# Row sums of squares for an RMS norm: from a transposed copy with adds and matmuls to the tokens' own layout with an accumulating activation

## The chip, the cores and the metric

The kernel runs on one core of one Trainium2 chip. The metric is the device time of one execution in microseconds (us); the figure for a version is the median of several runs. The engines are named as the profile names them: PE is TensorE (PEld its weight loads), DVE is VectorE, ACT is ScalarE, POOL is GpSimd, and SP is the engine whose queue issues most of the DMAs. Each engine, and the SP queue too, takes its instructions in the order in which the program lists them.

## The reference

One layer of a backbone over 2048 latent tokens and 256 context tokens, each a row of 1024 fp32 numbers. What matters here is its first step, cut from the reference:

```python
def _rmsnorm(x, g):
    xf = x.astype(jnp.float32)
    xf = xf * lax.rsqrt(jnp.mean(xf * xf, axis=-1, keepdims=True) + EPS)
    return (xf * g.astype(jnp.float32)).astype(x.dtype)
...
        mod = jax.nn.silu(c) @ w_ada[i] + b_ada[i]
        mod_c = jax.nn.silu(c_ctx) @ w_ada[i] + b_ada[i]
...
        h_lat = _rmsnorm(x, norm_g[i]) * (1.0 + scale) + shift
        h_ctx = _rmsnorm(ctx, norm_g[i]) * (1.0 + scale_c) + shift_c
...
    na_q, na_k, na_v, na_g, r_q, r_k, r_v, r_g = _split_proj(h_lat @ w_in)
```

So each token needs the sum of the squares of its own 1024 numbers before its row of h can be formed, and h is what the big projection h @ w_in reads. Behind it come neighbourhood attention, retention, an output projection and a last norm; the change does not touch those.

## The kernel before

**Groups and blocks.** The tokens are handled in nine groups of 256: group i = 0 to 7 is latent tokens, group 8 the context. A block is what the projection takes as one operand: blocks 0 to 3 are two groups each (block 2 is groups 4 and 5, block 3 is groups 6 and 7), block 4 is group 8. PE multiplies h in two parts: `hi`, a rounded copy (tiles `hhi`, and `chi` for the context), and `lo`, the rest (tiles `hlo`, `clo`). Both must be ready for a row block k of a block before PE can use it.

**What is done to a group.** Its data come transposed (features on partitions, tokens along the row) by `load_x`, two DMAs of 512 KB. Then, by the short names that the plan uses:

- `sq` squares: ACT squares both halves into two `st` tiles (L198); for one half POOL, for the other DVE adds the four feature blocks together (L200, L201), and DVE adds the two halves (L203).
- `cs` colsum: PE multiplies the result by a column of ones (L209), which sums over the partitions and leaves one sum for each token in PSUM.
- `rs` rstd and spread_copy: DVE scales the sum (L214), POOL takes the power -1/2 (L215), DVE copies it along a row (L220).
- `sp` spread: PE turns that into a row for every partition (L227, two matmuls of 128 for each group).
- `mu`: DVE multiplies the transposed data with it (L241). `ab`: DVE (L272) and ACT (L274) apply scale and shift. `hl`: ACT casts to `hi` (L279), POOL or DVE subtracts for `lo` (L283), and the raw data are queued to be stored to DRAM for a later pass (`spill_step`, L253). Groups 0 and 1 go through `p` (prep_first) instead, one feature block k at a time: cast on ACT (L262), scale and shift on DVE (L263), `lo` on DVE or POOL (L265).

**The order.** Nothing is reordered by a scheduler. PE works through five windows, one for each block (L363), a window having 32 steps of three matmuls of 512 columns. After step n (counted over all windows, so that window 1 begins with step 32, window 2 with 64, window 3 with 96) the program lists the actions whose entry in the table `PLAN` has this n: `(52, 'sq', 6)` puts the squares of group 6 behind step 52 on every engine that they use. The times at which an engine gets to them depend on what stands ahead of them in its own queue. The modulation matmuls over `w_ada` (`m`, L311, with `ar` and `af`) are in the same plan, for the first 16 steps. A finished unit of a window is cast by ACT (L383), its rest is taken by DVE (L384) and both go out by one DMA on SP (`kS`, L151). Of the `o` tiles for that there are two.

**Buffers and queues.** `st` tiles of 512 KB are four, taken in turn by weights, squares and the context data. The DMAs of SP are issued in program order, and each waits for the landing of the one eight places ahead of it in the queue.

Of the kernel before, what the change touches and what calls it, by code (L numbers as in the profile page):

```python
# [9 lines left out]
F32 = mybir.dt.float32  # L10
BF16 = mybir.dt.bfloat16
F32R = mybir.dt.float32r
AF = mybir.ActivationFunctionType
# [5 lines left out]
P = 128  # L19
# [39 lines left out]
]  # L59
SPL = [9, 0, 1, 0]  # L60
ALO = [0, 5, 9, 4]
# [21 lines left out]
def hybrid_kernel(ctx: ExitStack, tc: tile.TileContext, a: dict, out: bass.AP):  # L83
    nc = tc.nc
# [33 lines left out]
    def pool(st, name, bufs, **kw):  # L118
        return st.enter_context(tc.tile_pool(name=name, bufs=bufs, reuse_waits="tile", **kw))
# [9 lines left out]
    psm = pool(ctx, "psm", 2, space=PSUM)  # L129
    KH = KC // 2  # L130
    env = dict(pp=pool(psx, "pp", 6, space=PSUM), st=pool(sx, "st", 4, side="right"), queue=nc.sync)

    def ptile(p=None):
        return (p or env["pp"]).tile([P, 512], F32, name="mm")
# [23 lines left out]
    blk = [(hx.tile([P, KC, 512], F32R, name="hhi"), hx.tile([P, KC, 512], F32R, name="hlo"))] + [None] * 4  # L158
# [4 lines left out]
    xsq = [[xraw[4 + i][:, u * KH:(u + 1) * KH, :] for u in range(2)] for i in range(2)]  # L163
# [27 lines left out]

    sqs, rms, rbs, prs = {}, {}, {}, {}

    def squares(i):
        sqs[i] = []
        for u in range(2):
            sq = xsq[i][u] if i < 2 else env["st"].tile([P, KH, 256], F32, name="st")
            nc.scalar.activation(sq, raw[i][u], AF.Square)  # L198
            eng = (nc.gpsimd, nc.vector)[u]
            eng.tensor_tensor(sq[:, 0:2, :], sq[:, 0:2, :], sq[:, 2:4, :], ALU.add)  # L200
            eng.tensor_tensor(sq[:, 0, :], sq[:, 0, :], sq[:, 1, :], ALU.add)  # L201
            sqs[i].append(sq)
        nc.vector.tensor_tensor(sqs[i][0][:, 0, :], sqs[i][0][:, 0, :], sqs[i][1][:, 0, :], ALU.add)  # L203

    def colsum(*ii):
        pm = ptile(None if ii[0] < 4 else psm)
        for j, i in enumerate(ii):
            for t in range(2):
                nc.tensor.matmul(pm[:, 2 * j + t:2 * j + t + 1], sqs[i][0][:, 0, t * P:(t + 1) * P], one, start=True, stop=True)  # L209
            rms[i] = pm[:, 2 * j:2 * j + 2]  # L210

    def rstd(i):
        r = env["st"].tile([P, 2], F32, name="rs", bufs=4)
        nc.vector.tensor_scalar(r, rms[i], 1.0 / D, EPS, ALU.mult, ALU.add)  # L214
        nc.gpsimd.tensor_tensor(r, r, mhalf[:, 0:2], ALU.pow)  # L215
        rbs[i] = r

    def spread_copy(i):
        rbs[i, 1] = env["st"].tile([P, 2, P], F32, name="t0", bufs=2)
        nc.vector.tensor_copy(rbs[i, 1], rbs[i].unsqueeze(2).to_broadcast([P, 2, P]))  # L220

    def spread(*ii):
        pm = ptile()
        for j, i in enumerate(ii):
            prs[i] = pm[:, j * 256:(j + 1) * 256]
            for t in range(2):
                nc.tensor.matmul(prs[i][:, t * P:(t + 1) * P], rbs[i, 1][:, t, :], ident, start=True, stop=True)  # L227
# [10 lines left out]
    def spread_mul(i, uu=(0, 1)):  # L238
        for u in uu:
            x = raw[i][u]  # L240
            nc.vector.tensor_tensor(x, x, prs[i].unsqueeze(1).to_broadcast([P, KH, 256]), ALU.mult)  # L241
# [93 lines left out]
    def w_raw(c0):  # L335
        return st_halves(a["w_in"][c0 // WG])
# [14 lines left out]
    def w_split(rw, lo=3):  # L351
        w, parts = w_parts(rw, lo)
        for p in parts:
            p()
        return w
# [108 lines left out]
    lds = dict(a=ada_load, x=load_x, c=small, w=lambda g: wr.append(w_raw(512 + 256 * g)))  # L464
    for name, *args in LOADS:
        lds[name](*args)
    acts = dict(sq=squares, cs=lambda *i: colsum(*i), rs=lambda i: (rstd(i), spread_copy(i)), sp=lambda *i: spread(*i),
                mu=lambda i, u: spread_mul(i, (u,)), ab=prep_ab, hl=prep_hl, blk=alloc_blk, x=load_x, w=lambda: wr.append(w_raw(2560)),
                w2=lambda: load_w(), s=ada_split, m=ada_mm, ar=ada_row, af=ada_fin, p=prep_first,
                ws=lambda g: w01.append(w_split(wr[g], lo=WSL[g])))  # L470
# [16 lines left out]
    def load_w():  # L487
        if wseq:
            wcur.append(w_raw(wseq.pop(0)))
# [523 lines left out]
    def dims(t):  # L1013
        h, i, j = t // 16, t // 4 % 4, t % 4
        return h, i, j, KWIN[i][0], KWIN[i][1], CWIN[j][0], CWIN[j][1]
# [214 lines left out]
    for t in range(NT + 3):  # L1230
# [27 lines left out]
        h, i, j = dims(t)[:3]  # L1258
# [237 lines left out]
    q, r = divmod(48 - used, 7)  # L1496
# [127 lines left out]
```

## Time and profile before

| | us |
|---|---|
| median of three runs | 1363.7 |
| lowest and highest run | 1363.22, 1367.48 |
| the profiled execution | 1366.09 |
| its span, from the first to the last instruction | 1364.1 |

All times inside the profile count from the start of that span; 2.0 us of the profiled execution lie outside it, and it is 2.4 us above the median of the runs. In the lists of instructions a row gives start, length, engine, line, operation, out<-in, how many were merged, and in brackets the idle time of the engine just before it with what ended it. An engine name with q (SPq) means the issue of a DMA, not its transfer. PEclk is the share of the full TensorE clock that was granted.

### The profile page before, as it was taken

Reading aid. Unit: us, or ns where it says so; the run is one execution under the profiler, and the core shown is the slowest. Engines: PE = TensorE matmul, PEld = TensorE weight load, DVE = VectorE, ACT = ScalarE, POOL = GpSimd, SP = SyncE. Lnnn points to the kernel's source line nnn. Section 1 sums busy time; section 2 is a strip of 40 time slices with the busy share of each in tenths; the row PEclk is TensorE's granted clock in tenths of the full one; section 3 lists DMA queues with packets and bytes.
Section 4 is the critical chain, followed back from the end, with each engine's and each line's share of the span. In section 5 each row is a group of like instructions: output and inputs, shape, how many; then the busy total and the mean of one; then the engine's idle time right before and its main releaser. Section 6 shows DMA issues by size and latency. Waiting matters only on the chain.

```text
span 1364.1 us, 23087 instructions
## 1 busy us (share of the span) xinstructions
PE 1313.1 (96%) x8236; PEld 1148.9 (84%) x8236; DVE 827.9 (61%) x1442; ACT 606.5 (44%) x1259; POOL 583.8 (43%) x571
## 2 busy tenths in 40 slices
PE   6999999999999999999999999999999899999997
PEld 2477899887997788998999889889998789888886
DVE  5686356675766754377767777776644633445345
ACT  5354343243533344555655466556642234333332
POOL 5452102554034664355535465555422254544432
PEclk9999999999999999999999999999999999999999
DMA  9386788464867657967587778676538988455533
GB/s 364 132 277 232 260 296 222 165 208 151 326 179 228 217 197 230 273 198 194 157 225 208 210 202 245 171 215 188 140 110 277 267 264 286 159 170 170 162 121 128
DMA packets 197685, 287.25 MB, mean 211 GB/s; under 512 B 17345, under 2 KB 126017, under 8 KB 196290
## 3 DMA queue, kind: packets, MB, share of 16 engines
q1 hardware_dynamic: 165154, 228.35, 56.4%
q10 hardware_dynamic: 32416, 57.42, 11.7%
q8 instruction: 66, 1.08, 0.3%
q14 instruction: 49, 0.40, 0.1%
HBM read 194.48 MB, written 91.23 MB: 209 GB/s over the span
## 4 chain that ended last, share of the span: by engine, by line
PE 70%; DMA 9%; DVE 8%; ACT 4%; POOL 3%; issue 3%; SPq 2%; ACTq 0%; POOLq 0%; DVEq 0%
PE mm L374 17%; PE mm L671 13%; PE mm L1465 11%; PE mm L363 7%; PE sS L1025 4%; PE tr L1052 3%; PE po L1073 3%; PE mm L1188 2%; PE tr L1054 2%; PE po L1075 2%; DMA vB<-o 1%; PE mm L1377 1%; PE mm L1376 1%; PE mm L1375 1%; PE mm L311 1%
## 5 line engine op out<-in xcount | busy, mean ns | idle before, releaser
L374 PE MATMUL mm<-whi,hlo 128*128 128x256 f32 x832 | 228.5, 282 | 0.2 <-DMA hlo<-cS 0.2
L374 PE MATMUL mm<-whi,hhi 128*128 128x256 f32 x768 | 224.2, 292 | 0.0
L374 PE MATMUL mm<-wlo,hhi 128*128 128x256 f32 x768 | 216.9, 282 | 0.0
L1056 ACT CAST pt<-tr 128x640 fp32r<-128x640 f32 (+1 forms) x128 | 95.6, 747 | 160.9 <-PE tr L1054 158.4
L1062 DVE TENSOR_TENSOR pt<-tr,pt 128x640 fp32r<-128x640 f32 (+1 forms) x128 | 113.9, 890 | 78.5 <-ACT pt L1056 77.2
L374 PEld LDWEIGHTS mm<-whi,hlo 128*128 128x128 f32 x832 | 156.3, 190 | 0.6 <-DMA hlo<-cS 0.5
L1045 POOL TENSOR_SCALAR sp<-sp,stt 128x640 f32<-128x640 f32 (+2 forms) x128 | 103.2, 808 | 106.5 <-DVE stt L1044 74.5
L374 PEld LDWEIGHTS mm<-whi,hhi 128*128 128x128 f32 x768 | 146.2, 190 | 0.0
L374 PEld LDWEIGHTS mm<-wlo,hhi 128*128 128x128 f32 x768 | 145.9, 190 | 0.1
L1034 DVE CUSTOM_DVE_ANT_0 sp<-sS,nb 128x640 f32<-128x640 f32 (+2 forms) x128 | 105.6, 825 | 33.6 <-PE sS L1025 27.2
L1039 ACT ACTIVATE sp<-sp,stt 128x640 f32<-128x640 f32 (+2 forms) x128 | 107.4, 839 | 19.9 <-DVE stt L1034 18.7
L625 POOL TENSOR_TENSOR whi<-st,whi 128x512 fp32r<-128x512 f32 x48 | 63.9, 1353 | 107.3 <-ACT whi L624 107.3
L363 PE MATMUL mm<-hhi,whi 128*128 128x512 f32 x256 | 107.8, 421 | 0.0
L363 PE MATMUL mm<-hlo,whi 128*128 128x512 f32 x256 | 101.6, 397 | 6.0 <-DVE hlo L265 2.1
L1025 PE MATMUL sS<-k,q 128*128 128x256 f32 (+3 forms) x512 | 99.0, 315 | 5.3 <-DVE stt L1034 5.0
L363 PE MATMUL mm<-hhi,wlo 128*128 128x512 f32 x256 | 101.9, 398 | 0.3 <-DVE wlo L347 0.3
L671 PE MATMUL mm<-hhi,whi 128*128 128x512 f32 x336 | 98.4, 395 | 3.7 <-POOL whi L625 3.2
L1474 DVE TENSOR_TENSOR xt<-mm,xt 128x512 f32<-128x512 f32 x64 | 43.8, 686 | 87.4 <-PE mm L1465 87.3
L1465 PE MATMUL mm<-wor,y 128*128 128x512 f32 x384 | 95.6, 398 | 1.1 <-DVE xt L1474 1.1
L1025 PEld LDWEIGHTS sS<-k,q 128*128 128x128 f32 x512 | 82.7, 188 | 12.2 <-DVE stt L1034 8.4
L1465 PE MATMUL mm<-won,y 128*128 128x512 f32 x336 | 89.9, 406 | 0.0
L625 POOL TENSOR_TENSOR wlo<-st,wlo 128x512 fp32r<-128x512 f32 x36 | 53.6, 1488 | 77.4 <-ACT wlo L624 77.4
(258 smaller groups left out, 3057.5 us busy)
## 6 DMA issues: line engine op xcount, KB each, us to landing
st<-in_w_in_dram SPq DMA_DIRECT2D x64, 512.0 KB
q<-qS SPq DMA_DIRECT2D x64, 256.0 KB
hlo<-hS SPq DMA_DIRECT2D x20, 512.0 KB
k<-kS SPq DMA_DIRECT2D x16, 576.0 KB
kS<-o SPq DMA_DIRECT2D x16, 512.0 KB
vB<-o SPq DMA_DIRECT2D x64, 128.0 KB
qS<-o ACTq DMA_DIRECT2D x16, 512.0 KB
woS<-g ACTq DMA_DIRECT2D x32, 256.0 KB
```

The source lines that it names most:

```text
L363: nc.tensor.matmul(pm[:, :n], ww[:, k, cs], h[:, k, :], start=(k == 0 and i == 0), stop=(k == KC - 1 and i == 2))
L374: nc.tensor.matmul(pm[:, t * WG:(t + 1) * WG], h[:, k, o:o + P], ww[:, k, :], start=(k == 0 and i == 0), stop=(k == KC - 1 and i == 2))
L625: nc.gpsimd.tensor_tensor(t[:, 1], r, f(t)[:, 0], ALU.subtract)
L671: nc.tensor.matmul(pm, ww[:, k, :], hh[:, k, :], start=(k == 0 and i == 0), stop=(k == KH - 1 and i == 2))
L1025: nc.tensor.matmul(o, hd["q"][i][:, hl, j * P:(j + 1) * P], k, start=(hl == 0), stop=(hl == 1))
L1034: nc.vector.tensor_tensor_reduce(T["sp"][:, :n], T["s"], nbz[big][:, o:o + n], -1.0, 3e38, ALU.add, ALU.min, T["st"][:, 0:1])
L1039: nc.scalar.activation(sp[:, :n], sp[:, :n], AF.Exp, bias=st[:, 0:1], scale=-1.0, accum_out=st[:, 1:2])
L1045: nc.gpsimd.tensor_scalar(sp[:, :n], sp[:, :n], st[:, 2:3], 0.0, ALU.mult, ALU.add)
L1056: nc.scalar.copy(pt[:, :ng_ + 2, 0, :], tr[:, :ng_ + 2, :])
L1062: nc.vector.tensor_tensor(pt[:, :n, 1, :], tr[:, :n, :], f(pt)[:, :n, 0, :], ALU.subtract)
L1465: nc.tensor.matmul(pm, yy[:, k, :], ww[:, k, sl], start=(k == 0 and i == 0), stop=(k == 3 and i == 2))
L1474: nc.vector.tensor_tensor(xts[t][:, sl], pm, xts[t][:, sl], ALU.add)
```

## The change

For groups 2 to 8 the sums no longer come from the transposed data. A new action `xt` loads the group once more, from `x` (or `ctx`) in its own layout, tokens on partitions: two DMAs of 512 KB into `st` tiles. `sq` is then two ACT instructions, one for each 128 tokens, that square a row of 1024 in place and accumulate along it into one number per token. The adds of POOL and DVE and the matmuls with ones are gone for these groups, and so is `cs` in the plan; `rs` works in place on the accumulated sums. Groups 0 and 1 are as before. The transposed data are still loaded, because the multiplication needs them.

```diff
+    def load_xt_(i):
+        sqs[i] = []
+        src = a["ctx"] if i == 8 else a["x"][i * 256:(i + 1) * 256, :]
+        for t in range(2):
+            xt = env["st"].tile([P, KH, 256], F32, name="st").rearrange("p k t -> p (k t)")
+            nc.sync.dma_start(xt, src[t * P:(t + 1) * P, :])
+            sqs[i].append(xt)
+
     def squares(i):
+        if i >= 2:
+            rms[i] = env["st"].tile([P, 2], F32, name="rs", bufs=4)
+            for t, xt in enumerate(sqs[i]):
+                nc.scalar.activation(xt, xt, AF.Square, accum_out=rms[i][:, t:t + 1])
+            return
         sqs[i] = []
...
     def colsum(*ii):
-        pm = ptile(None if ii[0] < 4 else psm)
+        pm = ptile()
...
     def rstd(i):
-        r = env["st"].tile([P, 2], F32, name="rs", bufs=4)
+        r = rms[i] if i >= 2 else env["st"].tile([P, 2], F32, name="rs", bufs=4)
```

In the plan the `cs` entries of groups 2 to 8 are dropped, seven `xt` entries are added and three `sq` entries move; the rest stays in its order:

```diff
-    (31, 'sq', 5), (34, 'mu', 4, 1), (39, 'ab', 4, 0), (42, 'cs', 5), (42, 'rs', 5), (48, 'ab', 4, 1), (50, 'sp', 5),
-    (52, 'mu', 5, 0), (52, 'sq', 6), (53, 'x', 7), (53, 'blk', 2), (53, 'ab', 5, 0), (53, 'mu', 5, 1), (55, 'blk', 3),
...
+    (29, 'hl', 3, 1), (29, 'mu', 4, 0), (31, 'sq', 5), (34, 'mu', 4, 1), (39, 'ab', 4, 0), (42, 'rs', 5),
+    (46, 'xt', 6), (48, 'ab', 4, 1), (50, 'sp', 5), (52, 'mu', 5, 0), (52, 'sq', 6), (53, 'x', 7), (53, 'blk', 2),
```

The `xt` entries stand at steps 4 (groups 2 and 3), 11, 22, 46, 60 and 81 (groups 4 to 8). The `sq` entries of groups 2, 3 and 4 go from steps 5, 12 and 13 to 9, 10 and 17; those of groups 5 to 8 stay at 31, 52, 70 and 86.

Where this puts things, from the built programs. In the new program lines below the diff are 14 higher or so: squares are L207 (L198 before), the new loads L200, `load_x` L191 (L190), the stores `kS` L152 (L151) and `hS` L267 (L253), scale and shift on ACT L288 (L274), the cast to `hi` L293 (L279), the eviction L397 (L383).

The SP queue at the start, first before, then now. `clo` is the last of w_ada, `hlo` and `hhi` from `in_xT` are transposed groups 3, 4 and 5, `st<-in_x` the new loads:

```order
L190 DMA hlo<-in_xT_dram 128x1024 x2
L289 DMA clo<-in_w_ada_dram 128x1024
L190 DMA hhi<-in_xT_dram 128x1024 x4
L151 DMA kS_62<-o 256x1x512
L253 DMA hS_87<-hhi 128x4x256
```

The same place now:

```order
L191 DMA hlo<-in_xT_dram 128x1024 x2
L303 DMA clo<-in_w_ada_dram 128x1024
L200 DMA st<-in_x_dram 128x1024 x4
L191 DMA hhi<-in_xT_dram 128x1024 x2
L200 DMA st<-in_x_dram 128x1024 x2
L191 DMA hhi<-in_xT_dram 128x1024 x2
L200 DMA st<-in_x_dram 128x1024 x2
L152 DMA kS_62<-o 256x1x512
```

The loads for the squares of groups 2 and 3 now stand ahead of the transposed groups 4 and 5, and those of groups 4 and 5 between and behind them.

The SP queue in window 1, first before. `hS` are the stores of raw data of groups 0 to 3, `kS` finished units, `clo<-in_xT` is transposed group 7:

```order
L253 DMA hS_87<-hhi 128x4x256
L253 DMA hS_88<-hlo 128x4x256 x2
L151 DMA kS_61<-o 256x1x512
L253 DMA hS_88<-hlo 128x4x256 x2
L151 DMA kS_62<-o 256x1x512
L190 DMA clo<-in_xT_dram 128x1024 x2
L151 DMA kS_63<-o 256x1x512
```

The same place now:

```order
L267 DMA hS_87<-hhi 128x4x256
L267 DMA hS_88<-hlo 128x4x256 x2
L152 DMA kS_61<-o 256x1x512
L267 DMA hS_88<-hlo 128x4x256 x2
L200 DMA st<-in_x_dram 128x1024 x2
L152 DMA kS_62<-o 256x1x512
L191 DMA clo<-in_xT_dram 128x1024 x2
L152 DMA kS_63<-o 256x1x512
L200 DMA st<-in_x_dram 128x1024 x2
```

The new load for group 6 stands behind five stores of raw data, and one `kS` and the transposed group 7 now stand behind it; the load for group 7 comes after the next `kS`.

ACT in window 1, the squares of group 6 and what stands behind them, before (`chi` is the transposed group 6, `hhi` groups 4 and 5):

```order
L383 CAST o<-mm 128x512 x2
L274 ACTIVATE hhi<-hhi,mods 128x256 x2
L198 ACTIVATE st<-chi 128x1024 x2
L274 ACTIVATE hhi<-hhi,mods 128x256
L279 CAST hhi<-hhi 128x4x256 x3
L274 ACTIVATE hhi<-hhi,mods 128x256
L383 CAST o<-mm 128x512
```

And now:

```order
L397 CAST o<-mm 128x512 x2
L288 ACTIVATE hhi<-hhi,mods 128x256 x2
L207 ACTIVATE st,rs<-st 128x1024 x2
L288 ACTIVATE hhi<-hhi,mods 128x256
L293 CAST hhi<-hhi 128x4x256 x3
L288 ACTIVATE hhi<-hhi,mods 128x256
L397 CAST o<-mm 128x512
```

The place in the queue is the same; what the squares read is now the `st` tile of the new load instead of the transposed group.

More of the change, by code (lines that the diff above doesn't have):

```diff
@@ L192, in hybrid_kernel @@
     sqs, rms, rbs, prs = {}, {}, {}, {}
-    def squares(i):
+    def load_xt_(i):
[5 more added lines that the diff above has]
+            sqs[i].append(xt)
+    def squares(i):
+        if i >= 2:
[3 more added lines that the diff above has]
+            return
         sqs[i] = []
         for u in range(2):
-            sq = xsq[i][u] if i < 2 else env["st"].tile([P, KH, 256], F32, name="st")
+            sq = xsq[i][u]
             nc.scalar.activation(sq, raw[i][u], AF.Square)
@@ L466, in hybrid_kernel @@
         lds[name](*args)
-    acts = dict(sq=squares, cs=lambda *i: colsum(*i), rs=lambda i: (rstd(i), spread_copy(i)), sp=lambda *i: spread(*i),
+    acts = dict(sq=squares, xt=load_xt_, cs=lambda *i: colsum(*i), rs=lambda i: (rstd(i), spread_copy(i)), sp=lambda *i: spread(*i),
                 mu=lambda i, u: spread_mul(i, (u,)), ab=prep_ab, hl=prep_hl, blk=alloc_blk, x=load_x, w=lambda: wr.append(w_raw(2560)),
```

29 rows, old and new, of the table PLAN are left out of this document.

## The prediction

> **What bounds the kernel now.** I read the page's first part, then who PE waits for, then the granted clock and the DMA load by stretch (the share is busy time of the 16 DMA engines), then the queues row by row.
>
> ```profile
> PE 1313.1 (96%) x8236; PEld 1148.9 (84%) x8236; DVE 827.9 (61%) x1442; ACT 606.5 (44%) x1259; POOL 583.8 (43%) x571
> ```
>
> PE is busy for 96% of the span, so whatever moves PE in the first 130 us, where all of the change lies, moves the end. PE's longest waits there that the change can touch (total, times, longest):
>
> ```profile
> PE mm L363 <- DVE hlo L265: 2.1, 2, 1.7
> PE mm L363 <- DVE hlo L283: 2.0, 1, 2.0
> PE mm L227 <- DVE t L220: 1.5, 1, 1.5
> PE mm L363 <- POOL hlo L283: 1.5, 1, 1.5
> ```
>
> Each is a `lo` part or a norm that comes late from another engine, never a load.
>
> ```profile
> 38.69:42.11 3.42, 3.42 (x5) 0.44 (x4) 3.23 (x6) 0.00 (x0) 0.82 (x1) 0.50 1.03 410
> 45.00:69.00 24.00, 23.62 (x96) 13.06 (x95) 16.80 (x32) 11.01 (x18) 9.51 (x11) 1.00 0.01 3
> 76.24:79.65 3.41, 3.41 (x9) 2.62 (x9) 3.41 (x3) 2.31 (x3) 3.41 (x2) 0.50 0.97 249
> 73.30:100.00 26.70, 24.74 (x109) 20.15 (x108) 22.41 (x31) 14.64 (x21) 12.44 (x9) 0.94 1.03 344
> ```
>
> The last three numbers are granted clock, DMA share and GB/s. Behind the 1.7 us wait and the 2.0 us wait the clock stood at 0.50 for 3.4 us each: half of that, 1.7 us, is lost besides the wait. The DMA engines are idle from 45 to 69 us and full from 73 to 100 us.
>
> **The change, part by part. What goes.**
>
> ```profile
> L209 PE MATMUL mm<-one,st 128*128 128x1 f32 x28 | 3.6, 238 | 0.4 <-DVE st L203 0.4
> L200 POOL TENSOR_TENSOR st<-st 128x512 f32<-128x512 f32 x7 | 10.4, 1483 | 13.2 <-ACT st L198 13.2
> ```
>
> PE's 28 column-sum records are 3.6 us, 0.5 us a group. POOL and DVE lose their adds for seven groups.
>
> **Front, to the start of window 1.**
>
> ```profile
> 33.76 0.40 DVE L263 TENSOR_SCALAR hhi<-hhi,mods 128x256 f32<-128x256 f32 x1
> 35.53 1.37 DVE L263 TENSOR_SCALAR hhi<-hhi,mods 128x256 f32<-128x256 f32 x1
> 36.93 0.90 DVE L265 TENSOR_TENSOR hlo<-hhi 128x256 fp32r<-128x256 f32 x1
> 35.28 1.46 POOL L200 TENSOR_TENSOR st<-st 128x512 f32<-128x512 f32 x1
> 37.88 0.50 PE L363 MATMUL mm<-hlo,whi 128*128 128x512 f32 x1 [1.70 <-DVE hlo L265]
> 38.54 3.46 PE L311 MATMUL mm<-hlo,silc 128*2 128x512 f32 x4
> 54.24 1.88 PE L311 MATMUL mm<-clo,silc 128*2 128x512 f32 x4
> 20.36 1.61 SPq L190 DMA_DIRECT2D hlo<-in_xT_dram  x2
> 31.94 4.10 SPq L190 DMA_DIRECT2D hhi<-in_xT_dram  x4
> 35.64 1.08 ACT L262 ACTIVATE hhi<-hhi,mods 128x256 fp32r<-128x256 f32 x2
> 47.92 0.39 PE L363 MATMUL mm<-hhi,whi 128*128 128x512 f32 x1
> ```
>
> The DVE row at 35.53 takes 1.37 us instead of the 0.40 of the one at 33.76, while POOL's add at 35.28 runs. Without that add, `lo` is there about 1.4 us sooner, PE's 1.7 us wait shrinks to 0.3, and the halved clock behind it (four matmuls in 3.46 us against 1.88) goes: 1.4 + 1.6 = -3.0 us. But the squares of group 2 now read a load that takes the slot issued at 31.94, where transposed group 4 was. That slot waits for the landing of the DMA eight ahead, the second one of the row at 20.36 (issued at about 21.6): 10.3 us from issue to landing with the queue full. So the new halves land at 42.2 and 43.5, the squares end at 44.7 (1.0 us for the second, by ACT's row at 90.55 below, and a 0.2 us accumulator read), and the two casts of feature block k = 3, behind them on ACT, end at 45.8 instead of 36.7 (the row at 35.64); DVE and POOL need some 1.1 us more for `lo`. PE needs that at step 12 (the row at 47.92), which it would reach 3.0 us sooner, at 44.9: with `lo` at 46.9 it waits about 2.0 us. The column sums of groups 2 and 3 are -1.0. Front: -3.0 + 2.0 - 1.0 = **-2.0**; between -4.0 (the casts hidden) and 0 (the new wait also halves the clock). The 2.0 us wait at window 1 (for DVE L283) stays, with its clock: the chain of waits to it runs from the norms of groups 2 and 3 over DVE's L241 and L272, with no add in it, so it only moves along with the front; group 4's column sum lies ahead of this wait and yields nothing. Groups 4 and 5 cost nothing here: at 1.28 us a DMA (31.94 to the end of four issues) their loads land from 50 to 56 us, about when ACT, eight plan steps behind the casts of k = 3, wants the first; their transposed halves, 5 us later than before, are first multiplied by DVE well into window 1.
>
> **Accumulating.**
>
> ```profile
> L1039 ACT ACTIVATION_READ_ACCUMULATOR sp<-sp,stt 128x1 f32 x128 | 24.1, 189 | 0.0
> ```
>
> Elsewhere an activation that accumulates is followed by a 0.19 us read. Fourteen make 2.7 us on ACT, which is 44% busy; only 0.2 us behind a late load counts.
>
> **Start of block 2 (step 64).** This is the term that decides.
>
> ```profile
> 85.34 2.29 SPq L253 DMA_DIRECT2D hS<-hlo  x2
> 87.73 1.35 SPq L151 DMA_DIRECT2D kS<-o  x1
> 89.12 2.75 SPq L253 DMA_DIRECT2D hS<-hlo  x2
> 91.97 1.33 SPq L151 DMA_DIRECT2D kS<-o  x1
> 93.40 2.59 SPq L190 DMA_DIRECT2D clo<-in_xT_dram  x2
> 110.74 5.57 DMA hS<-hhi
> 156.50 9.82 DMA kS<-o
> 90.55 1.99 ACT L198 ACTIVATE st<-chi 128x1024 f32<-128x1024 f32 x2
> 92.81 0.60 ACT L274 ACTIVATE hhi<-hhi,mods 128x256 f32<-128x256 f32 x1 [0.27 <-DVE hhi L241]
> 93.32 1.98 ACT L279 CAST hhi<-hhi 128x1024 fp32r<-128x1024 f32 x2
> 95.38 2.46 POOL L283 TENSOR_TENSOR hlo<-hhi 128x1024 fp32r<-128x1024 f32 x1 [1.25 <-ACT hhi L279]
> 99.20 3.27 POOL L283 TENSOR_TENSOR hlo<-hhi 128x1024 fp32r<-128x1024 f32 x1 [1.37 <-ACT hhi L279]
> 102.53 0.50 PE L363 MATMUL mm<-hlo,whi 128*128 128x512 f32 x1 [1.45 <-POOL hlo L283]
> ```
>
> SP issues back to back from 85 us, one 512 KB DMA in 1.2 to 1.4 us, because the DMA engines take no more. The load for group 6's squares comes behind the stores that end in the row at 89.12, so its halves take the slots 91.97 and 93.40, and the `kS` and group 7 there move behind it. From issue to landing the chain shows 5.6 and 9.8 us for two stores; for the crowded queue I take 6.5, nearer to the first because the second stood behind a burst of weight loads. The second half lands at 99.9. ACT reaches these squares at 90.55 and takes nothing else meanwhile: squares end at 101.1 (1.0 + 0.2), L274 0.5, three casts 3 x 0.99 = 104.6. POOL's two subtractions (2.46 and up to 3.27) start behind the second cast, at 103.6, and end near 109.1. PE's `lo` comes at 109.1 instead of 102.5: **+6.6**, from +4.5 (5.6 us to land, 2.46 twice) to +10 (9.8 us). DVE's adds for groups 5 to 8 count as nothing, since what is late next is ACT. The `kS` that is now two slots later keeps its `o` tile longer, but the eviction that wants the tile (L383) is queued on ACT behind the same squares; transposed group 7, as much later, belongs to block 3 and is not multiplied before window 2.
>
> A wait of 8 us leaves the clock at half for one or two stretches of 3.4 us, of which some 3.4 us lie in work: **+1.7** (0 to +3.4). PE's 1.5 us wait for `t` (L227) is covered by this one: **-1.5**. The column sums of groups 5 and 6 lie ahead of the wait and yield nothing; group 7's gives **-0.5**.
>
> **Start of block 3 (step 96).**
>
> ```profile
> 122.32 1.58 SPq L253 DMA_DIRECT2D hS<-chi  x2
> 121.00 2.17 ACT L198 ACTIVATE st<-st 128x1024 f32<-128x1024 f32 x2
> 127.81 2.35 DVE L283 TENSOR_TENSOR hlo<-clo,hhi 128x1024 fp32r<-128x1024 f32 x2
> 129.89 0.40 PE L363 MATMUL mm<-hlo,whi 128*128 128x512 f32 x1
> ```
>
> The context's new load takes the two slots from 122.32 on, in the time of before, since the `kS` ahead of it waits for an eviction that PE places. That queue is not jammed (two issues in 1.58 us), so I take 5 us to land, a little under the 5.6: the second half, issued at 123, is there at 128, and ACT, which reaches these squares at 121.0, ends them at 129.2. An eviction, scale and shift and a cast (0.5 + 1.0 + 1.0) and DVE's subtraction (1.2) bring `lo` of group 7 at 132.9, 3.0 us after the row at 129.89, where PE wants it: **+3.0** (0 to +4; group 8's column sum lies ahead of it), and in half of such cases a halved clock, **+0.9**.
>
> Sum: -2.0 + 6.6 + 1.7 - 1.5 - 0.5 + 3.0 + 0.9 = +8.2 us. Behind block 3 PE sets the pace and passes this on. The profiled execution's 1366.1 would become 1374.3; it is 2.4 us above the median, 1363.7, which becomes 1371.9. Two waits can overlap more than I let them, so I say 1371.
>
> [...]
>
> **The rivals.** *Faster: the squares never hold ACT.* If the second half for group 6 lands by 92 us, PE's wait at step 64 vanishes (-1.5), L227's too (-1.5), column sums of groups 5 to 8 count (-2.0), and with the front's -2.0 the time is 1356.7. For it: `xt` stands six steps ahead of `sq`, and the DMA engines are idle until 69 us. Against it: the rows from 85.34 to 93.40, a jam that puts the landing 8 us too late. The sum is zero with a landing near 93 us (nothing lost at block 2, the rest as forecast), or near 96 if block 3 hides its wait too. *Within 0.3%.* The load lands some 3 us sooner because the queue drains faster with loads than with stores (+3.6 instead of +6.6, no clock loss), and block 3's chain is hidden: -2.0 + 3.6 - 1.5 - 0.5 = -0.4, 1363.3. For it: two of the ten DMAs in the jam change from stores to loads. Against it: loads and stores were issued there at the same 1.3 us. Anything from 1359.6 to 1367.8 counts here. *Slower still.* The new wait at step 12 halves the clock as well (+1.7), block 2's landing is nearer 9.8 us (+3): 1376. For it: 7 MB more pass the DMA engines in the first 130 us. Against it: most of them pass where the engines were idle.
>
> **How the numbers follow.** A difference of 0.3%, 4.1 us, is about what a measurement of this kernel can tell from none. The forecast and its slower form 0.66 together (0.08 of it above 1377), within 0.3% 0.20, faster 0.14. The range 1360 to 1377 leaves out the faster case and that tail; the forecast's own range is 1367 to 1377.
>
> **What would show it.** Right: ACT's squares of group 6, near 90 us, have an idle gap of 5 us or more ahead of them, ended by the DMA `st<-in_x`, PE waits 6 us or more in all at the start of window 2, the clock is halved behind it, and the first granted 0.50 near 39 us is gone. The second jam shows as ACT waiting for `st<-in_ctx`. Wrong: ACT reads group 6 without a gap; then the faster case holds. If the new rows at 42 to 47 us show no wait at step 12, the front was under-rated.

## The result, and the profile after

The changed kernel takes 1385.7 us (median of four runs, 1380.5 to 1388.2), the kernel before 1364.5 (1363.2 to 1367.5): ratio 1.0145, interval 1.0124 to 1.0165. Run once more beside later experiments it took 1387.3 us, ratio 1.0165 (1.0145 to 1.0184); over all eight runs the median is 1387.0. It is slower by 21 us or a little more; the forecast was slower by 8. The profiled execution took 1380.5 us, with a span of 1378.7, and is the fastest of its four; so the trace shows 14 of the 21 us.

The starts of some steps on PE, in us, from the timelines of both traces:

| step | before | changed | difference |
|---|---|---|---|
| 32 (window 1) | 73.66 | 73.16 | -0.5 |
| 63 (last of window 1) | 99.91 | 98.38 | -1.5 |
| 72 (block 2 under way) | 111.48 | 118.17 | +6.7 |
| 95 | 128.95 | 135.17 | +6.2 |
| 100 (block 3 under way) | 132.91 | 149.75 | +16.8 |
| 127 | 151.89 | 168.73 | +16.8 |

All of the loss lies at two places, steps 64 and 96. Behind step 127 2.2 us come back and the rest is passed on. How long that last stretch takes varies by itself: the kernels of this document don't differ there, and in the sixteen profiles it takes from 1204.6 to 1216.6 us (1212.2 before, 1210.0 here). The page's busy times, and whom PE waited for between 20 and 150 us (total, times, longest):

```profile
PE 1313.6 (95%) x8208; PEld 1148.6 (83%) x8208; DVE 814.6 (59%) x1421; ACT 607.3 (44%) x1273; POOL 566.0 (41%) x557
```

```profile
PE mm L377 <- ACT hhi L293: 14.4, 3, 6.8
PE mm L377 <- POOL hlo L297: 3.1, 1, 3.1
PE mm L377 <- DVE hlo L297: 2.9, 3, 1.5
PE mm L377 <- DVE hlo L279: 1.6, 3, 1.0
```

The work is what it was: PE 1313.6 us busy against 1313.1, DVE and POOL 13 and 18 us less. What is new is 14.4 us of waiting for ACT's casts to `hi`. The rows of PE, ACT and SP at step 64:

```profile
105.98 0.80 PE L377 MATMUL mm<-hhi,whi 128*128 128x512 f32 x1 [6.75 <-ACT hhi L293]
109.90 0.79 PE L377 MATMUL mm<-hlo,whi 128*128 128x512 f32 x1 [3.13 <-POOL hlo L297]
...
90.07 1.09 ACT L288 ACTIVATE hhi<-hhi,mods 128x256 f32<-128x256 f32 x2
100.06 1.06 ACT L207 ACTIVATE st<-st 128x1024 f32<-128x1024 f32 x1 [8.90 <-DMA st<-in_x_dram]
101.46 1.06 ACT L207 ACTIVATE st<-st 128x1024 f32<-128x1024 f32 x1 [0.24 <-DMA st<-in_x_dram]
103.00 2.92 ACT L293 CAST hhi<-hhi 128x1024 fp32r<-128x1024 f32 x3
...
89.99 2.75 SPq L267 DMA_DIRECT2D hS<-hlo  x2
92.78 2.63 SPq L200 DMA_DIRECT2D st<-in_x_dram  x2
95.93 0.53 SPq L152 DMA_DIRECT2D kS<-o  x1
```

ACT comes to the squares of group 6 at 91.2 and has nothing else to take. Their load was issued at 92.78 and 94.2, behind the last store, and is there at 100.06 and 101.46; the casts of group 5, behind the squares on ACT, start at 103.0, and PE, at the end of window 1 by 99.2, stands until 109.9 with one matmul between. At step 96 the same picture comes twice:

```profile
111.51 1.48 SPq L200 DMA_DIRECT2D st<-in_x_dram  x2
113.04 0.46 SPq L267 DMA_DIRECT2D hS<-hhi  x1
...
131.57 0.52 SPq L152 DMA_DIRECT2D kS<-o  x1
132.13 1.48 SPq L200 DMA_DIRECT2D st<-in_ctx_dram  x2
...
117.21 1.06 ACT L207 ACTIVATE st<-st 128x1024 f32<-128x1024 f32 x1 [5.28 <-DMA st<-in_x_dram]
126.31 1.05 ACT L293 CAST hhi<-chi 128x1024 fp32r<-128x1024 f32 x1 [2.30 <-DMA hS<-hhi]
137.73 1.06 ACT L207 ACTIVATE st<-st 128x1024 f32<-128x1024 f32 x1 [6.82 <-DMA st<-in_ctx_dram]
...
142.63 0.80 PE L377 MATMUL mm<-hhi,whi 128*128 128x512 f32 x1 [6.60 <-ACT hhi L293]
144.45 0.79 PE L377 MATMUL mm<-hlo,whi 128*128 128x512 f32 x1 [1.03 <-DVE hlo L297]
```

Group 7's load holds ACT for 5.3 us, a store that was pushed behind that load holds a cast for 2.3 (1.2 before), the context's load holds ACT for 6.8. From within both waits of PE to some us behind them the clock is halved, for 13.65 and 10.24 us (in the rows below, the busy us of PE, PEld, DVE, ACT and POOL, then PEclk, DMA share and GB/s); in the parts of these in which PE worked, 6.0 and 5.6 us by its busy times, half is lost, 3.0 and 2.8 us by this estimate (matmuls of 512 columns start 0.43 us apart at 111 us, 0.23 at 117, where the clock is at 1.00 again).

```profile
101.45:115.10 13.65, 6.00 (x13) 4.42 (x14) 9.05 (x9) 6.97 (x10) 5.43 (x3) 0.50 0.47 157
139.00:149.24 10.24, 5.58 (x14) 4.28 (x15) 4.58 (x8) 4.97 (x8) 0.70 (x1) 0.50 0.54 195
```

At the front most of the forecast came in this execution: no 0.50 near 39 us, a new wait at step 12 of 0.39 and 0.96 us (2.0 forecast), and step 63 1.5 us sooner (2.0 forecast).

### The profile page after: what moved, and what is told of

It is laid out like the page before. It is cut to its first block, busy times and chain, and to the rows that moved or that the text cites. A ratio compares the mean times of both kernels' runs of the same rounds, so it can differ in the third digit from the quotient of the medians.

```text
span 1378.7 us, 23014 instructions
## 1 busy us (share of the span) xinstructions
PE 1313.6 (95%) x8208; PEld 1148.6 (83%) x8208; DVE 814.6 (59%) x1421; ACT 607.3 (44%) x1273; POOL 566.0 (41%) x557
## 3 DMA queue, kind: packets, MB, share of 16 engines
q8 instruction: 65, 1.06, 0.3%
## 4 chain that ended last, share of the span: by engine, by line
PE 68%; DMA 10%; DVE 8%; issue 4%; ACT 4%; POOL 4%; SPq 2%; ACTq 0%; POOLq 0%; DVEq 0%
PE mm L388 16%; PE mm L685 13%; PE mm L1479 11%; PE mm L377 5%; PE sS L1039 5%; PE tr L1066 3%; PE po L1087 3%; DMA kS<-o 2%; PE tr L1068 2%; PE mm L1202 2%; PE po L1089 2%; DMA v<-rvS 1%; PE mm L325 1%; PE mm L1390 1%; PE mm L1389 1%
## 5 line engine op out<-in xcount | busy, mean ns | idle before, releaser
L377 PE MATMUL mm<-hhi,whi 128*128 128x512 f32 x256 | 109.3, 427 | 14.8 <-ACT hhi L293 14.4
L377 PE MATMUL mm<-hlo,whi 128*128 128x512 f32 x256 | 103.0, 402 | 8.0 <-POOL hlo L297 3.1
L1479 PEld LDWEIGHTS mm<-wor,y 128*128 128x128 f32 x384 | 70.5, 190 | 19.6 <-issue 3.5
```

The source lines that it names most:

```text
L377: nc.tensor.matmul(pm[:, :n], ww[:, k, cs], h[:, k, :], start=(k == 0 and i == 0), stop=(k == KC - 1 and i == 2))
L1479: nc.tensor.matmul(pm, yy[:, k, :], ww[:, k, sl], start=(k == 0 and i == 0), stop=(k == 3 and i == 2))
```

## The experiments

Each run was compared with the kernel before on the same chip. The theory is that of the prediction: ACT takes its queue in order, and a load for squares that stands behind stores on SP holds everything behind the squares. Against it stand the traffic itself and the new instructions.

| kernel | median us | ratio to before | interval |
|---|---|---|---|
| changed | 1387.0 (eight runs) | 1.0145, 1.0165 | 1.0124 to 1.0184 |
| group 6's load early | 1377.1 | 1.0087 | 1.0067 to 1.0106 |
| groups 6 and 7 early | 1371.0 | 1.0047 | 1.0029 to 1.0065 |
| groups 6, 7 and context early | 1371.4 | 1.0040 | 1.0021 to 1.0059 |
| no loads | 1357.3 | 0.9945 | 0.9926 to 0.9964 |
| seven loads unread | 1363.4 | 0.9995 | 0.9981 to 1.0008 |
| group 7's load unread | 1362.7 | 0.9988 | 0.9975 to 1.0002 |
| squares of 6 and context later | 1364.0 | 1.0002 | 0.9985 to 1.0018 |
| squares of 6 later | 1373.6 | 1.0089 | 1.0059 to 1.0118 |
| squares of context later | 1374.1 | 1.0075 | 1.0049 to 1.0102 |
| squares of 2 and 3 behind casts | 1382.0 | 1.0122 | 1.0100 to 1.0143 |
| filler matmuls in the waits | 1383.0 | 1.0127 | 1.0105 to 1.0148 |
| loads ahead of the stores | 1359.3 | 0.9965 | 0.9946 to 0.9983 |
| the same, group 5 behind casts | 1357.6 | 0.9950 | 0.9933 to 0.9968 |

**The price of the instructions, of the loads, and of waiting for them.** Two kernels change one line, so that ACT squares what is there anyway; in the first of them the `xt` entries go too, and in a third only that of group 7 comes back.

```diff
-            for t, xt in enumerate(sqs[i]):
+            for t, xt in enumerate([u.rearrange("p k t -> p (k t)") for u in raw[i]]):
```

> The seven loads are left out; ACT squares and accumulates in place on the transposed data that are there anyway (so the sums are not the norm's; the same instructions, the same place, the same sizes). It prices the change without its loads. Place theory and traffic theory alike: 1356 to 1361, with ACT waiting for no load. Instruction theory (the accumulating squares, with the 0.19 us read behind each, or the power of POOL in their chain, cost the time): 1370 or more.

> The seven loads are there, in the same places of the SP queue as in the changed kernel, but nobody reads them: ACT squares and accumulates in place on the transposed data (the sums are not the norm's). Place theory in its narrow form (ACT's wait is the whole cost): within 2 us of the kernel without loads. Queue rival (the loads push the stores and the transposed loads behind them, and late stores hold the hhi and o tiles): the stores of raw data and kS come two slots later and the kernel is 6 us or more slower than the one without loads. Traffic theory: near 1380.

> The kernel without loads (sums over the transposed data, 1357.3) with one of the seven put back, unread: that of group 7, behind a kS and ahead of the four stores of raw data of groups 4 and 5 and the two kS among them. Queue rival: it pushes these stores by 2.5 us, ACT's cast of group 6 (hhi<-chi), which waits for the hhi tile to be stored, comes as much later, PE waits 2 to 4 us at step 96 as with all seven unread, and the median is 1361 to 1364. If it is group 6's load that pushes (kS and transposed group 7), nothing of this shows and the median is 1357 to 1359.

Without loads: 1357.3, 7 us faster than before. The accumulating squares, and the adds and matmuls that are gone, are a gain. The seven loads, unread, take 6 us of it by the medians, and group 7's alone 5 of these; by the traces, step 127 comes 4.9 and 2.6 us later than without loads. The reason is one cast of ACT, into an `hhi` tile whose old content must have been stored; without loads, then with the one, then with all three late loads early:

```profile
112.78 1.05 ACT L293 CAST hhi<-chi 128x1024 fp32r<-128x1024 f32 x1 [3.46 <-DMA hS<-hhi]
```

```profile
115.41 1.05 ACT L293 CAST hhi<-chi 128x1024 fp32r<-128x1024 f32 x1 [6.10 <-DMA hS<-hhi]
```

```profile
120.44 1.05 ACT L293 CAST hhi<-chi 128x1024 fp32r<-128x1024 f32 x1 [7.09 <-DMA hS<-hhi]
```

With group 7's load alone the cast comes 2.6 us later, and PE then waits 1.5 and 1.3 us at step 96, where without loads it waits 0.5. So the queue rival holds for 6 us. The other 23 us, from 1363.4 to 1387.0, with the same DMAs in the same order on SP, come only from ACT reading what they bring, the wait at the front included: neither traffic nor instructions.

**The order on ACT.** All loads stay where they are, late as they are; only squares move behind the casts of the group ahead, both pairs, or one of them (with the context's go its norm and its spread, `rs` and `sp`, which need them).

```diff
-    ... (52, 'sq', 6), ... (86, 'sq', 8), ... (92, 'rs', 8), ... (96, 'sp', 8),
+    ... (61, 'sq', 6), ... (95, 'sq', 8), (96, 'rs', 8), ... (106, 'sp', 8),
```

> The changed kernel with all loads left where they are; only two pairs of squares move: group 6's behind ACT's casts of group 5 (step 52 to 61), the context's behind its casts of group 7 (step 86 to 95, with its spread at 106). So the loads land as late as before, but fewer instructions are queued on ACT behind them. Theory (the cost is ACT's order behind a late load, the lateness itself is harmless): no wait over 2 us at step 64, the wait at step 96 is that of the kernel with unread loads (2.3 + 1.3 us, from pushed stores), median 1362 to 1367. If the late sums themselves are wanted at once (spread of group 6 at step 68), the wait only moves to there and the median stays at 1375 or more.

> Only half of the edit that brought the changed kernel to 1364: the squares of group 6 behind ACT's casts of group 5 (step 52 to 61); those of the context stay. Block 2's share alone is taken away. If the loss is block 2's 6 to 8 us and block 3's 10, as the traces say, the wait at step 64 is gone, ACT still waits some 7 us for the context's load ahead of the scale and shift of group 7, PE waits 7 us at step 96: median 1372 to 1378. If the late start of block 2 is what makes block 3 late (one loss that is handed on), the wait at step 96 goes too: 1364 to 1368.

> The other half: the squares of the context behind ACT's casts of group 7 (step 86 to 95, spread at step 106); those of group 6 stay. Block 3's share alone is taken away: PE's 9.9 us at step 64 stay, the 7.6 us at step 96 fall to 4 us or less (what the stores that were pushed leave), median 1375 to 1380. If the load of group 7 and the pushed stores are what holds block 3, step 96 keeps 6 us or more and the median is 1382 to 1387.

Both: 1364.0, as before the change. The rows of ACT at step 64, then PE's longest waits between 20 and 150 us:

```profile
95.33 2.94 ACT L293 CAST hhi<-hhi 128x1024 fp32r<-128x1024 f32 x3
...
104.30 1.06 ACT L207 ACTIVATE st<-st 128x1024 f32<-128x1024 f32 x1
...
111.01 1.06 ACT L207 ACTIVATE st<-st 128x1024 f32<-128x1024 f32 x1 [4.06 <-DMA st<-in_x_dram]
```

```profile
PE mm L241 <- DVE t L234: 4.2, 3, 1.5
...
PE mm L377 <- ACT hhi L293: 1.1, 1, 1.1
```

The casts pass at 95.3 instead of 103.0. ACT still waits 4.1 us for group 7's load, but what is queued behind it isn't wanted yet, and PE's 14.4 us of waiting for casts is 1.1. The wait at step 96 that the unread loads leave, 2.3 and 1.3 us, was expected here too and isn't there; what makes the two kernels alike in time is that this one keeps the late front (step 32 at 74.9 us instead of 71.0). In the changed kernel ACT stood idle for 8.9 us ahead of the squares, to 100.06, though the casts behind them can start at 95.3, as they do here: in this pair of kernels ACT keeps to the order of its queue, and the places of these few instructions are worth 23 us (1387.0 less 1364.0). The two halves:

```profile
PE mm L377 <- ACT hhi L293: 7.2, 2, 6.2
```

```profile
PE mm L377 <- ACT hhi L293: 8.6, 2, 7.5
```

The first is with group 6's squares moved: the wait at step 96 stays (6.2 us). The second is with the context's moved: the wait at step 64 stays (7.5), and step 96 comes without any wait, less than the 4 us expected; the median, 1374.1, is 1 us under its range. The halves take the ratio from 1.0155 (mean of the two) to 1.0089 and 1.0075, which is 9 and 11 us, and both together take 21: within the intervals, some 3 us each, the shares add.

**The place of the loads.** In steps: group 6's load from 46 to 22; that and group 7's from 60 to 46; all, with the context's from 81 to 60.

> Only the load for the squares of group 6 moves: from step 46 to step 22, directly behind that of group 5, into the stretch in which the DMA engines idle. Place theory (what costs is that loads for squares stand behind stores on SP and ACT waits for them in order): the 8.9 us wait of ACT ahead of the squares of group 6 goes, PE's 6.8 + 3.1 us at step 64 shrinks to 2 us or less, and step 72 comes about 7 us sooner than the changed kernel's 118.2 us. The loads of group 7 and of the context still stand behind a kS that waits for an eviction, so ACT still waits for them and step 100 loses about as much as it did: median 1374 to 1380. Traffic theory (7 MB more through the DMA engines slow everything in the first 150 us, wherever they stand): 1383 to 1388, with longer times from issue to landing elsewhere.

> Loads of groups 6 and 7 early (steps 22 and 46), the context's load left at step 81. It parts the loss at step 96. If the context's load is its cause (ACT waited 6.8 us for it with only group 6 early, ahead of the scale and shift and the casts of group 7): the wait of PE at step 96 stays at 6 us or more, median 1374 to 1377, close to the 1377.1 of group 6 alone. If group 7's load is (squares 5 us late, stores pushed): the wait falls to 3 us or less and the median to 1369 to 1372, that of all three early.

> All three late loads move one place forward: group 6 to step 22, group 7 to step 46, the context to step 60. Place theory: every load lands before ACT wants it, ACT waits for no load of x or ctx from 60 us on, PE's waits at steps 64 and 96 are 2 us or less in all, and the gain of the front and of the adds is left: median 1357 to 1363, faster than before. Traffic theory: the same 7 MB pass, so 1375 or more.

Group 6's load early does what moving its squares did (1.0087 and 1.0089). All three early miss their range, 1371.4 against 1357 to 1363: from 60 us on ACT waits for no load there, but the context's load now stands ahead of the stores of `hhi` (the cast at 120.44 above), and PE waits 2.5 and 1.3 us at step 96. Of the 10.3 us by which step 127 comes later in this trace than without loads, 6.2 are lost from step 95 to 100 and 3.8 by step 32, by the front with its clock halved.

With groups 6 and 7 early the trace and the time part. Two rows of ACT, and PE's longest wait for a cast:

```profile
118.04 1.05 ACT L293 CAST hhi<-chi 128x1024 fp32r<-128x1024 f32 x1 [4.45 <-DMA hS<-hhi]
...
129.21 1.06 ACT L207 ACTIVATE st<-st 128x1024 f32<-128x1024 f32 x1 [6.57 <-DMA st<-in_ctx_dram]
```

```profile
PE mm L377 <- ACT hhi L293: 8.3, 2, 7.2
```

ACT waits 6.6 us for the context's load and PE 7.2 us at step 96, as expected if that load is the cause, but the median is 6 us below that of group 6 alone, which the other theory expected. The traces don't show these 6 us where the two kernels differ: step 127 comes at 160.4 us, with group 6 alone at 159.6. The span is 4.9 us shorter all the same, by what lies behind step 127 (1210.9 and 1216.6 us). Nor do the medians show that all three early take 4.1 us less from step 95 to 100. What the 6 us are stays open.

**The front.** Only the squares of groups 2 and 3 move, behind the casts for step 12.

```diff
-    (9, 'sq', 2), (9, 'p', 3), ... (10, 'sq', 3), ... (12, 'p', 5), ... (12, 'p', 4),
+    (9, 'p', 3), ... (12, 'p', 5), ... (12, 'p', 4), (12, 'sq', 2), (12, 'sq', 3),
```

> The changed kernel with the squares of groups 2 and 3 moved behind the casts of k = 3 to 5 (step 12), nothing else. PE's 1.4 us wait at step 12 goes and step 32 comes 1.5 to 3 us sooner. If the wait at step 64 ends at a time that the DMA queue sets, this gain is gone at step 72: median 1384 to 1387, as the changed kernel. If waits add up as the forecast's sum let them, it stays: 1381 to 1383.

The wait at step 12 is gone and step 32 comes 2.0 us sooner (71.20). In the trace most of that is lost again at step 64: steps 72 and 127 are 0.8 us sooner. The median, 1382.0, is 5 us lower, with intervals that overlap, and lies where it was expected if the gain stays (1381 to 1383); the trace speaks for the other expectation. The wait at step 12 costs more in other executions than in the profiled one: of nine profiles of kernels that have it, six show a halved clock behind it, which the two of the changed kernel don't. Two of the six, the kernel with both squares later and the one with the context's:

```profile
48.51:51.92 3.41, 3.41 (x8) 0.63 (x7) 2.42 (x8) 2.71 (x7) 1.18 (x2) 0.50 1.04 412
```

```profile
47.96:54.78 6.82, 6.28 (x12) 1.73 (x13) 5.17 (x12) 5.50 (x11) 1.56 (x2) 0.50 1.03 410
```

**The clock.** Filler matmuls run while PE waits.

```diff
+            if b in (2, 3) and n == 0:
+                fill = ptile(psm)
+                for _ in range(40 if b == 2 else 32):
+                    nc.tensor.matmul(fill, w01[0][0][:, 0, 0:P], blk[1][0][:, 0, :], start=True, stop=True)
```

> The changed kernel with filler matmuls in PE's two long waits: 40 matmuls of 512 columns (about 9 us) ahead of step 64 and 32 (about 7 us) ahead of step 96, into a spare PSUM tile that nobody reads. The waits end when they did, but PE isn't idle in them. Clock theory (the halved clock behind the two waits cost 3.0 and 2.8 us of the time): no granted 0.50 near 101 to 115 and 139 to 149 us, steps 64 to 72 and 96 to 104 shorter by about 3 us each, median 1379 to 1382 against 1385.7. If the halved clock is hidden (what follows waits for DMAs anyway): 1384 or more.

Steps 96 to 104 without the fillers, then with them:

```profile
142.60:151.90 9.30, 8.24 (x26) 6.39 (x27) 3.16 (x4) 1.40 (x2) 0.34 (x1) 0.64 0.47 168
```

```profile
147.00:154.50 7.50, 6.32 (x29) 4.89 (x28) 3.17 (x4) 1.15 (x2) 0.09 (x1) 1.00 0.55 196
```

The clock stays at 1.00, and step 104 comes 7.5 us after step 96 instead of 9.9. At step 64 one stretch of 3.4 us at 0.50 is left, at 114 us, and step 72 comes 10.2 us after step 64 instead of 12.2. The median is 4 us lower than the changed kernel's, with intervals that overlap; 1379 to 1382 was expected. The trace bears out the halved clock as a part of the loss; its size, 4 us by the medians, 4.4 by these two stretches and 5.8 by the busy times above, is not settled.

**The changed kernel again.**

> The changed kernel itself, once more, for a second profile and more runs beside those of this call: its four runs lay from 1380.5 to 1388.2 us at almost the same mean clock (0.983 to 0.987), and the profiled one was the fastest. If the extra 4 to 8 us of the others are longer waits in the first 150 us, a slower profile shows PE idle for more than the 17.5 us in all that it had at steps 64 and 96. Median 1383 to 1388.

The second profile (1383.8 us, again the fastest of its four) has 18.5 us of waits at steps 64 and 96 against 17.5, and half a microsecond more at step 12, but step 127 comes only 0.2 us later: 3.1 of the 3.3 us by which its span is longer lie behind it. So the expectation that longer waits in the first 150 us make the slower runs is not borne out by these two. What the runs near 1388 add was not caught in a profile. Three runs show a lower mean clock, 0.983 instead of 0.987, which by estimate, from 0.004 of the span, is 11 us more at half clock or up to 5 us lost; others at 0.987 are as long.

**A version that is faster than both.** The new loads of groups 5 to 7 go ahead of all stores, into the stretch in which the DMA engines are idle (a share of 0.00 from 60 to 70 us in the changed kernel); ACT squares where it was idle; the squares of groups 2 and 3 go behind the casts as in the front experiment; the context's load goes behind its transposed one and its squares to step 95. In the second version group 5's squares move from step 17 to 20, behind the casts of k = 7 and 6.

```diff
+    (11, 'xt', 5), ... (12, 'p', 4), (12, 'sq', 2), (12, 'sq', 3), ... (17, 'sq', 4), (17, 'sq', 5), ... (22, 'xt', 6), (22, 'xt', 7),
+    ... (31, 'sq', 6), (31, 'sq', 7), ... (79, 'x', 8), (79, 'xt', 8), ... (95, 'sq', 8), (96, 'rs', 8), ... (106, 'sp', 8),
```

> All loads for squares of x leave the stretches in which stores crowd SP. Group 5 goes to step 11, groups 6 and 7 to step 22, so all of them issue before 60 us, while the DMA engines idle; to free the st tiles, ACT squares group 5 at step 17 (it was idle for 8 us there) and groups 6 and 7 at step 31, ahead of an 6 us idle gap; the squares of groups 2 and 3 stand behind the casts of k = 3 to 5, and the context's load moves behind its transposed load (step 79) with the squares at step 95. Place theory with the queue rival's part (loads must neither be waited for nor push stores): no wait of PE over 1 us at steps 12, 64 and 96, median 1352 to 1358, as fast as the kernel without the loads (1357.3) or faster. If ACT's four more squares ahead of the casts of groups 2 and 3 hold those up, PE's wait at step 32 grows beyond the 2.5 us it has and the median is 1360 to 1365.

> The kernel with the loads ahead of the stores, with one pair moved: the squares of group 5 behind the casts of k = 6 and 7 (step 17 to 20). There PE waited 1.9 us at step 23 for a lo part that came late because ACT waited for the load of group 5. Expected: that wait goes, step 32 comes 1 to 1.5 us sooner, median 1357 to 1359.5. If the squares now hold up scale and shift of groups 2 and 3 instead, it is the same or up to 1 us slower.

The first is 1359.3, 0.35% faster than before, 1 us over the range: it kept a wait of 1.9 us at step 23, for the squares of group 5. The second has lost that too and is 1357.6, 0.5% faster than before and level with the kernel without loads. What PE still waits for in it:

```profile
PE mm L377 <- DVE hlo L297: 1.5, 1, 1.5
PE mm L377 <- POOL hlo L297: 1.4, 1, 1.4
PE mm L377 <- ACT hhi L293: 1.2, 1, 1.2
```

## Why the prediction was wrong in size

The direction and the mechanism were right: the squares behind a late load, PE's `lo` at 109.9 us where 109.1 was worked out, the gap on ACT of 8.9 us, the halved clock behind it. 1385.7 lies above the range that ended at 1377. In parts:

- **Block 2, nearly right.** The terms were +6.6, +1.7 for the clock and -1.5 for the wait for `t`; taking the place away alone, which brings back a 1.5 us wait for `t`, is worth 9 us (0.66%), where these terms make 6.8. The load took 7.2 us from issue to landing where 6.5 was taken, the clock cost 3.0 us instead of 1.7 (0.50 for four times 3.41 us, where the estimate was one or two), and PE's first and longer wait was for `hi`, the last of the three casts, at 105.98. In the trace steps 63 to 72 take 8.2 us more than before.
- **Block 3, the step that failed: +3.9 forecast, 10.6 in the trace, 11 by the experiment.** The prediction let the context's load take "the two slots from 122.32 on, in the time of before, since the `kS` ahead of it waits for an eviction that PE places". But ACT places this eviction. PE had finished its unit by 124.6 us (117.5 before), and the eviction started at 129.34 (119.52 before), 4.7 us later instead of 2.0: on ACT it stood behind the squares that waited for group 7's load, 5.3 us, and behind a cast that waited 2.3 us for a store (1.2 before), and that store stood behind group 7's new load. The sum has no term for either. So the `kS` went out at 131.57 instead of 121.74, and the load came at 137.7 and 139.0. ACT, free for the squares at 130.9, waited 6.8 us, about the 6.3 that the forecast's own times give; but PE was ready for step 96 5.1 us after ACT was free, where it had been 8.7 us in the profile before (129.65 less 121.00). PE's wait was 7.6 us instead of 3.0, and the halved clock, 10.24 us of it, cost 2.8 instead of 0.9.
- **What block 3 doesn't need.** Neither the late block 2 nor group 7's late load is a necessary cause. With block 2 repaired and the context's squares left, the wait at step 96 is still 6.2 us. With the loads of groups 6 and 7 early ACT waits for neither, and steps 95 to 100 still take 15.0 us (14.6 in the changed kernel, 4.0 before): there the cast waits 4.5 us for its store, though the last new load ahead of that store was issued some 10 us sooner, and the eviction starts 5.2 us after PE has finished its unit. Why that store lands late is not shown. In all seven profiles with the context's load and squares at these places ACT waits 6.6 to 6.8 us for the load; in the six of them without filler matmuls PE is ready 4.3 to 5.7 us after ACT is free. The failed step is thus the meeting of ACT, SP and PE in the times of the old profile; group 7's load is one way in which ACT falls behind PE, and not the only one.
- **The front, -2.0 forecast.** In the three profiles of this front in which the clock stays whole behind step 12, step 24 comes 1.7 to 1.9 us sooner, much as forecast. Step 32 comes only 0.4 to 0.5 us sooner, because a new wait of 1.1 us for a cast of ACT stands ahead of its first matmul, and step 63 1.4 to 1.5. In the six with the halved clock step 32 comes 1.2 to 3.4 us later (74.8 to 77.1) and step 63 0.5 to 2.7; the mean of the nine at step 63 is +0.3. That was the rival "slower still", named and priced at +1.7, with too little weight. Moving those squares is worth 4 to 5 us by the medians, though not outside the intervals. The sum also booked the front's 2 us as a gain and let block 2's wait end at a time that the queue sets; in the trace of the front experiment such a gain is swallowed (2.0 us at step 32, 0.8 at step 72), while its median doesn't bear that out.
- **The rivals that fell.** "The squares never hold ACT" was 1356.7; without the waits the change does give 1357.3 to 1357.6, so its price was right in sum and its condition wasn't met. In its parts that is luck: without loads PE's wait at step 64, which it let vanish, is still 1.3 us, and the front gains more than its 2.0 (step 63 comes 3.5 us sooner than before). Two loads that drain faster and hide: no sign of it.

Put together, of the 13 us by which the forecast was too low, 7 are block 3, about 2 the front and 2 block 2, and 2 are not placed; with intervals of some 3 us on each, no more exact sum is to be had.

## What to carry to other kernels

A transfer that replaces arithmetic is placed by the queue it stands in, not by the step at which it is listed (here group 6's load went out at 92.78 us, behind the last store, and was there at 100.06): read what its queue issues just then, and where it lands against the moment its reader comes to it and against the moment the reader's work is wanted. Where the reader's engine takes its work in order, as ACT did here, the cost is everything queued behind the reader; moving the reader behind the urgent work repaired that here, 1387.0 to 1364.0 us, though the loads stayed late. And when a first wait delays the end of a window, work the next window through with every queue moved, not in the times of the old profile.

## What the runs showed of the hardware that was not expected

The same wait has a halved clock behind it in some executions and not in others. At step 32 all fifteen profiles with the new squares show the same two idle gaps of PE, 1.05 to 1.22 and 1.48 to 1.50 us (1.06 and 1.48 in the changed kernel), and behind them the clock is at 0.50 for 3.41 us in eight and at 1.00 in seven. Up to the last one, which runs on past the program's end, the stretches at 0.50 are 3.41, 3.41 and 6.83 us long in the profile before, and 13.65, 10.24, 3.41 and 3.41 us in that of the changed kernel: one, two, three or four times 3.41. Within each of the two profiles their starts lie whole multiples of 3.41 us apart (38.69 and 76.24 before, 101.45 and 139.00 changed: 37.55 us both times, eleven times 3.41). What sets these multiples, and whether the place of a wait between them decides, is not shown. At step 12 the clock stood at 1.00 behind gaps of up to 1.9 us in all (1.35 in the first profile of the changed kernel) and at 0.50 behind 2.2 us or more; but before the change 0.50 followed a single gap of 1.70 us (PE at 37.88), so the length of a gap alone does not tell.

The twelve runs of the kernel with all three loads early lie from 1364.4 to 1379.0 us, 24 runs of the kernel before beside it from 1361.0 to 1369.0; but the eight of the changed kernel, which has such waits too, spread no more than those (1380.5 to 1389.0). That the clock makes the spread is not shown. One profile is one draw: the stretch behind step 127, in which the kernels don't differ, takes up to 12 us more in one of the sixteen than in another.
